# A two-block transformer kernel: a zeroed margin moved ahead of the loads, pooling read some ticks after GpSimd starts it, and the sums of w_ada spread differently over three stages

## The chip, the cores and the metric

The kernel runs on 1 core of one Trainium2 chip, as one launch. Its time is the device time of the whole program in microseconds (us); smaller is better. Before the change the median of 3 runs is 2774.2 us (2769.51 to 2774.95).

## The reference, cut to what matters

All arrays are float32, batch 1, 256 tokens, model width 2048. Two different transformer blocks run one after the other, each once.

```
h = rms_norm(x, pre_mix_g);  q, k, v, u = split(h @ w_in)        # 4 x 1024 columns
a = chunked_attention(q, k, v, rel_bias)                         # 8 heads of 128
p = multiscale_pool(u): group g = 0..3 (256 channels each):
        trailing mean over 2, 4, 8, 16 tokens, minus the token;  then @ pool_w[g], * pool_scale
x = x + rms_norm(concat(a, p) @ w_o)
x = x + rms_norm((gelu(conv(h @ w_up)[:5632]) * conv(..)[5632:]) @ w_down)   # first feed-forward

shift1, scale1, gate1, shift2, scale2, gate2 = split(silu(c) @ w_ada + b_ada, 6)     # also for c_ctx
hc = rms_norm(ctx) * (1 + cscale1) + cshift1;   h = rms_norm(x) * (1 + scale1) + shift1
keys and values from hc and h (512 rows), queries and gates from h (256 rows)
x = x + gate1 * merge(two attentions);  x = x + gate2 * swiglu(rms_norm(x) * (1 + scale2) + shift2)
```

w_ada is 2048 x 12288. Its product with a vector is computed on VectorE as dot products of rows, not on TensorE.

## The kernel before, in words

**Tokens and weights.** A float32 product is made of three matmuls on a rounded high part and a low part. Each weight slab is 128 x 1024 (512 KB, two half slabs): SyncE loads it into one of 4 tiles `w`, ScalarE casts it to `h` (L237), VectorE subtracts to get `l` (L238), both with 5 buffers, and TensorE uses it. `Stream.prep` issues these for the next slab as soon as TensorE's uses of the oldest one stand in the program. Every engine works through its own queue strictly in the order in which the Python code calls it, so this order is written out by hand.

**Side work.** Everything else in a stage (heads, pooling, norms) is written as generators in `Side`. A *tick* comes after each half slab; on a tick, at most `per` of the active generators that are due go on to their next `yield n`, which asks to be left alone for n ticks. At most `limit` are active, the rest wait in a queue.

**The sums of w_ada.** `Stream.vitems` holds 192 loads of 128 x 1024 of w_ada into two tiles `v` (L211, GpSimd's queue), and VectorE makes dot products of each with a broadcast row of silu(c) that lies in `adat` (L536, called a sum here). The first 64 loads have two sums each (c and c_ctx: "kind 0", 128 sums), then 32 loads each for shift2, gate1, scale2, gate2 with one sum each. `Stream.done` adds `pace` to a credit after each half slab and takes one sum per whole credit, up to `limit` loads; `PACE` has a pair per stage (feature-major and token-major products). After a sum that was a tile's last, the tile's next load is issued at once behind it. `ada_begin` loads the rows (L510) and lets the first sum come 8 ticks later.

**Block 1** (`block1`): norm of x, then v, q, k for heads 0 to 3 (`qkproj`), u (`uproj`), the other halves, pooling's mixing (`mix`), and the output projection. VectorE copies a zeroed margin of `ut` into the zero parts of the probabilities (L654). GpSimd's queue loads the condition `cc`, sends its silu to DRAM (`crow`, L626), loads the rows, then the table of biases `rb`, sets a part of the table to -1e30 (L651) and clears the margin (L652). `pool(g)` adds shifted copies on GpSimd (L666; 1, 2, 3, 4 additions for g = 0..3), and directly behind them VectorE corrects the start, scales, subtracts and splits (L669 to L676).

**First feed-forward** (`ffn1`): six groups of hidden columns, and in `ctx_norm` the norm of the context, which begins when kind 0 is summed. **Keys' stage** (start of `block2`): six chunks of 512 columns over four row tiles with 7 banks of PSUM; keys (chunks 0, 2, 3) are normed on VectorE (L1159 to L1190) before their bank is free. Then come queries, attention, merging and the second feed-forward.

Of the kernel before, what the change touches and what calls it, by code (L numbers as in the profile page):

```python
# [22 lines left out]
AF = mybir.ActivationFunctionType  # L23
# [3 lines left out]
P = 128  # L27
# [5 lines left out]
GROUPS = [range(g, min(g + 8, NFB)) for g in range(0, NFB, 8)]  # L33
NEG = -1e30

PACE = ((0.3, 0.35), (0.19, 0.33), (0.0, 0.88), (0.0, 0.3), (0.1, 0.13))

ROWS = 8

# [231 lines left out]
class Kernel:  # L271
# [275 lines left out]
    def ada_end(self, names, kind):  # L547
        nc = self.nc
        if names[0] == "gate":
            self.side.urgent.append((self.side.now + 3, lambda: self.gate_row(kind)))  # L550
            return
        for name, dst, g in (("sc1", self.g1, "norm1_g"), ("csc1", self.gc1, "norm1_g"), ("sc2", self.g2, "norm2_g")):
            if name in names or any(name in n for n in names):
                nc.vector.scalar_tensor_tensor(dst, self.ada_v[name], 1.0, self.vec(g), op0=ALU.add, op1=ALU.mult)
        self.ada_done.update(range(4 * kind, 4 * kind + 4 * len(names)))
# [41 lines left out]
    def block1(self):  # L597
# [22 lines left out]
        self.meet(self.norm_b(start(0), 0, hh, hl))  # L620
        xs1 = start(1)
        first = self.token_major([(hh, hl, 0), (hh, hl, 1)], self.staged(lambda: self.norm_t(xs1, 1, hh, hl)))
        cc = self.small[:32]
        nc.gpsimd.dma_start(cc, a["cc"])
        nc.scalar.activation(cc, cc, AF.Silu)
        nc.gpsimd.dma_start(self.crow.rearrange("o (j p) -> (o j) p", p=P), cc)  # L626
        self.pace = PACE[0]
        self.ada_begin({0: 0, 1: 2}, 64)

        _, ah, al = self.pair(2)  # L630
        qk = self.slot(4, F32R).rearrange("p (s k t) -> p s k t", s=4, k=4)
# [13 lines left out]
        def half():  # L645
            zk[0] += 1
            return xq[2 + zk[0] % 2]
        self.half = half
        nc.gpsimd.dma_start(tab, a["rb"])
        nc.gpsimd.dma_start(inv, a["inv"])  # L650
        nc.gpsimd.memset(tab[0:64, :, 192:256], NEG)  # L651
        nc.gpsimd.memset(ut[:, :, :16], 0.0)  # L652
        for i in range(4):
            nc.vector.tensor_copy(pt[:, i % 2, i // 2, 1, :P], ut[:, :8, :16])  # L654

        def pool(g):

            w = 2 ** (g + 1)
            src = ut[:, 2 * g:2 * g + 2, :]
            cur, step = src, 1  # L660
            bufs = [pa, pb]
            while step < w:
                dst = bufs.pop(0)
                bufs.append(dst)
                n = 2 * step - 1
                nc.gpsimd.tensor_add(dst[:, :, n:], cur[:, :, n:], cur[:, :, n - step:272 - step])  # L666
                cur, step = dst, 2 * step
            fix = self.stat(32).rearrange("p (k t) -> p k t", k=2)
            nc.vector.tensor_mul(fix, cur[:, :, 16:32], inv[:, g * 16:(g + 1) * 16].unsqueeze(1).to_broadcast([P, 2, 16]))  # L669
            m = bufs[0]  # L670
            nc.vector.tensor_scalar_mul(m[:, :, 32:], cur[:, :, 32:], 1.0 / w)
            nc.vector.tensor_copy(m[:, :, 16:32], fix)
            nc.vector.tensor_sub(m[:, :, 16:], m[:, :, 16:], src[:, :, 16:])
            ph, pl = pooled(g)
            nc.scalar.copy(ph, m[:, :, 16:])
            nc.vector.tensor_sub(pl, m[:, :, 16:], ph.bitcast(F32))  # L676
            pool_done.add(g)
            yield 1
# [85 lines left out]
            state["v"] += 1  # L764

        vout(first)
        qkproj(0)
        qkproj(1)
        state["qk"] = 1
# [146 lines left out]
    def ffn1(self, pair, x, mid):  # L916
# [58 lines left out]
        def chunk_end(gi, c, t, bank):  # L975
            if gi == 2 and c == t == 0:
                side.add(self.ctx_norm(ch, cl))
            last = gi == len(GROUPS) - 1
            yc = y[:, t, c * 512:(c + 1) * 512]
            if gi == 0:  # L980
                nc.scalar.copy(yc, bank)
            else:
                nc.vector.tensor_add(yc, bank, yc)
            if last:
                self.sumsq(yc, ss[t][:, c:c + 1])
                nc.vector.tensor_mul(yc, yc, self.pfg[c])
            if gi == len(GROUPS) - 2 and c == 3 and t == 1:
                side.drain()
                S.finish()
                side.drain()  # L990
                assert S.vdone == 64 and len(self.ada_done) == 8
                for n in range(4):
                    nc.gpsimd.dma_start(self.pfg[n], a["pfg"][:, n * 512:(n + 1) * 512].to_broadcast([P, 512]))
            if last and c == 3 and t == 1:
                self.gtop = self.gbase + 1024 + 2048
                xs8 = [self.xs_[:, :512], self.xs_[:, 512:]] + [self.g(512) for _ in range(6)]
                S.fill()
                side.add(normed(xs8))
# [116 lines left out]
    def block2(self):  # L1115
# [49 lines left out]
        for c in range(6):  # L1165
            if c == 0:
                banks = self.token_major(toks, [
                    self.seg(range(8)), self.seg(range(8, KB), (0, 1), True, after=lambda: side.until(lambda: 0 in self.normed)),
                    self.seg(range(8, KB), (2,), True, after=lambda: (side.until(lambda: 1 in self.normed), side.add(tables()))),
                    self.seg(range(8, KB), (3,)), self.seg(range(8), (2, 3))])  # L1170
                side.until(lambda: "done" in tabs)
                used = [(self.oi + i) % 4 for i in range(1, 5)]
                self.obanks, self.sbanks, self.oi = used + [4, 5, 6], [7], 3
                self.pace = PACE[2]
                self.ada_begin({0: 0, 1: 1}, 128)
                (qtab_a, qtab_b), (ktab_a, ktab_b) = tabs["q"], tabs["k"]
            else:
                banks = self.token_major(toks, [self.seg(range(KB), range(4))])
            is_k, hd = c in (0, 2, 3), 128 if c < 2 else 64
            v = lambda z: z.rearrange("p (h d) -> p h d", d=hd)  # L1180
            rk = [heads_ss(banks[0], hd, hd, 1.0 / hd)] if is_k else None
            for i in range(4):
                if is_k and i < 3:
                    rk.append(heads_ss(banks[i + 1], hd, hd, 1.0 / hd))
                out = tmp()
                if not is_k:
                    nc.scalar.copy(out, banks[i])
                else:
                    y = tmp()
                    nc.vector.tensor_mul(v(y), v(banks[i]), rk[i].unsqueeze(2).to_broadcast([P, 512 // hd, hd]))  # L1190
                    if i < 2:
                        gn = self.hg[:, 128:256] if hd == 128 else self.hg[:, 320:384]
                        nc.vector.tensor_mul(v(out), v(y), gn.unsqueeze(1).to_broadcast([P, 512 // hd, hd]))
                    else:
                        self.rope(out, y, ktab_a if hd == 128 else ktab_b, i - 2, hd, tmp())
                nc.gpsimd.dma_start(kv[c][:, i, :], out)
# [383 lines left out]
```

## Time and profile before

| | us |
|---|---|
| median of 3 runs (lowest, highest) | 2774.2 (2769.51, 2774.95) |
| the profiled execution | 2776.85 |
| its span, first to last instruction | 2775.1 |
| TensorE (PE) busy with matmuls | 2699.4 (97%) |
| VectorE (DVE) busy | 2015.8 (73%) |
| ScalarE (ACT) busy | 1336.8 (48%) |
| GpSimd (POOL) busy | 248.8 (9%) |
| mean granted TensorE clock | 0.993 |

How to read it: the rows shown further down are whole lines of the profile. Times are us from the span's start unless marked ns. Idle time in front of an instruction stands in brackets with the engine, tile and line that ended it. Matmul records overlap, so a busy PE is not a PE at its peak; a granted clock (PEclk) of 1.00 is 2.4 GHz, and while it is 0.50 the array runs at 1.2 GHz. L12 is line 12 of the kernel.

### The profile page before, as it was taken

Reading aid. Unit: us, or ns where it says so; the run is one execution under the profiler, and the core shown is the slowest. Engines: PE = TensorE matmul, PEld = TensorE weight load, DVE = VectorE, ACT = ScalarE, POOL = GpSimd, SP = SyncE. Lnnn points to the kernel's source line nnn. Section 1 sums busy time; section 2 is a strip of 40 time slices with the busy share of each in tenths; the row PEclk is TensorE's granted clock in tenths of the full one; section 3 lists DMA queues with packets and bytes.
Section 4 is the critical chain, followed back from the end, with each engine's and each line's share of the span. In section 5 each row is a group of like instructions: output and inputs, shape, how many; then the busy total and the mean of one; then the engine's idle time right before and its main releaser. Section 6 shows DMA issues by size and latency. Waiting matters only on the chain.

```text
span 2775.1 us, 36806 instructions
## 1 busy us (share of the span) xinstructions
PE 2699.4 (97%) x13654; PEld 2274.2 (82%) x13654; DVE 2015.8 (73%) x2938; ACT 1336.8 (48%) x1994; POOL 248.8 (9%) x395
## 2 busy tenths in 40 slices
PE   7989899999999999998999999999999999999999
PEld 6878788888888887777777788888878888888887
DVE  5878787888887767767577877778766666665566
ACT  5444455545455645321256655644454444444443
POOL 1010000000000000222211100011000000000000
PEclk9999999999999999999999999999999999999999
DMA  7666667676776765666855544489857777766565
GB/s 264 199 217 230 241 211 259 220 251 215 244 238 207 227 191 168 232 245 243 292 178 178 171 155 156 148 322 322 274 170 227 236 230 233 234 198 195 185 205 166
DMA packets 167573, 608.91 MB, mean 219 GB/s; under 512 B 19472, under 2 KB 19664, under 8 KB 166368
## 3 DMA queue, kind: packets, MB, share of 16 engines
q1 hardware_dynamic: 127728, 461.43, 49.6%
q0 software_dynamic: 39520, 144.87, 15.8%
q8 instruction: 107, 1.75, 0.3%
q14 instruction: 74, 0.61, 0.1%
q10 hardware_dynamic: 144, 0.25, 0.0%
HBM read 591.76 MB, written 14.71 MB: 219 GB/s over the span
## 4 chain that ended last, share of the span: by engine, by line
PE 78%; DVE 3%; DMA 3%; ACT 2%; issue 2%; POOL 0%; DVEq 0%; ACTq 0%; POOLq 0%
PE bank L359 34%; PE bank L392 14%; PE bank L393 13%; PE bank L395 13%; DMA v<-wada 3%; PE bank L342 1%; DVE l L238 1%; PE bank L343 1%; PE bank L344 1%; PE bank L1275 1%; ACT h L237 1%; DMA G<-kv 0%; ACT G L477 0%; PE bank L452 0%; DVE G L536 0%
## 5 line engine op out<-in xcount | busy, mean ns | idle before, releaser
L238 DVE TENSOR_TENSOR l<-w,h 128x1024 fp32r<-128x1024 f32 x870 | 1059.9, 1225 | 357.6 <-ACT h L237 346.8
L237 ACT CAST h<-w 128x1024 fp32r<-128x1024 f32 x870 | 908.9, 1051 | 615.8 <-PE bank L393 430.9
L359 PE MATMUL bank<-pair,h 128*128 128x512 f32 x3072 | 842.8, 395 | 6.5 <-DVE slot L338 3.5
L359 PEld LDWEIGHTS bank<-pair,h 128*128 128x128 f32 x3072 | 526.7, 189 | 76.4 <-issue 3.7
L392 PE MATMUL bank<-h,pair 128*128 128x512 f32 x1344 | 539.3, 401 | 24.1 <-DVE slot L1190 10.3
L393 PE MATMUL bank<-h,pair 128*128 128x512 f32 x1344 | 530.0, 394 | 2.1 <-DVE G L426 1.4
L359 PEld LDWEIGHTS bank<-pair,l 128*128 128x128 f32 x3072 | 470.1, 189 | 66.6 <-DVE l L238 0.8
L359 PE MATMUL bank<-pair,l 128*128 128x256 f32 x3072 | 488.1, 281 | 0.1
L395 PE MATMUL bank<-l,pair 128*128 128x512 f32 x1344 | 416.0, 395 | 6.0 <-DVE l L238 5.9
L536 DVE CUSTOM_DVE_ANT_0 G<-v,G 128x1024 bf16<-128x1024 f32 x256 | 327.8, 1280 | 70.5 <-DMA v<-wada 68.8
L392 PEld LDWEIGHTS bank<-h,pair 128*128 128x128 f32 x1344 | 256.5, 191 | 83.5 <-issue 16.3
L395 PEld LDWEIGHTS bank<-l,pair 128*128 128x128 f32 x1344 | 255.3, 190 | 64.0 <-DVE l L238 9.5
L393 PEld LDWEIGHTS bank<-h,pair 128*128 128x128 f32 x1344 | 256.3, 191 | 53.6 <-DVE G L426 1.8
L392 PE MATMUL bank<-h,slot 128*128 128x512 f32 x768 | 299.1, 390 | 1.0 <-ACT slot L337 1.0
L393 PE MATMUL bank<-h,slot 128*128 128x512 f32 x768 | 299.0, 389 | 0.0
L395 PE MATMUL bank<-l,slot 128*128 128x512 f32 x768 | 237.7, 389 | 0.0
L211 POOL DMA_DIRECT2D v<-wada x192 | 102.1, 532 | 1337.7 <-DVE G L536 1281.0
L367 ACT COPY G<-bank 128x256 f32<-128x256 f32 x192 | 71.6, 373 | 278.5 <-PE bank L359 278.2
L392 PEld LDWEIGHTS bank<-h,slot 128*128 128x128 f32 x768 | 144.2, 188 | 30.8 <-ACT slot L337 1.5
L393 PEld LDWEIGHTS bank<-h,slot 128*128 128x128 f32 x768 | 144.2, 188 | 30.4 <-DVE slot L338 0.5
L395 PEld LDWEIGHTS bank<-l,slot 128*128 128x128 f32 x768 | 144.1, 188 | 30.0
L368 DVE TENSOR_TENSOR G<-bank,G 128x256 f32<-128x256 f32 x192 | 81.1, 422 | 109.4 <-ACT G L367 109.1
(217 smaller groups left out, 1700.4 us busy)
## 6 DMA issues: line engine op xcount, KB each, us to landing
v<-wada POOLq DMA_DIRECT2D x192, 512.0 KB, 4.8
w<-wup SPq DMA_DIRECT2D x176, 512.0 KB, 4.3
w<-wgu SPq DMA_DIRECT2D x176, 512.0 KB, 4.0
w<-wdn SPq DMA_DIRECT2D x88, 512.0 KB, 4.5
w<-wfd SPq DMA_DIRECT2D x88, 512.0 KB, 4.1
w<-w SPq DMA_DIRECT2D x66, 512.0 KB, 4.5
w<-w2g SPq DMA_DIRECT2D x64, 512.0 KB, 3.5
w<-w2kv SPq DMA_DIRECT2D x52, 512.0 KB, 4.4
```

Of the source, the lines that this page charges most:

```text
L211: self.nc.gpsimd.dma_start(t, src)
L237: self.nc.scalar.copy(h, w)
L238: self.nc.vector.tensor_sub(l, w, h.bitcast(F32))
L342: t.matmul(out, ah, bh, start=start, stop=False)
L343: t.matmul(out, ah, bl, start=False, stop=False)
L359: t.matmul(bank[:, :size], w[:, j * P:(j + 1) * P], x[:, kb, :size], start=s == n == 0, stop=s == 3 and n == 7)
L367: self.nc.scalar.copy(z, bank[:, 256:])
L368: self.nc.vector.tensor_add(out, bank[:, :256], z)
L392: self.nc.tensor.matmul(banks[i], xh, h, start=seen[i] == 1, stop=False)
L393: self.nc.tensor.matmul(banks[i], xl, h, start=False, stop=False)
L395: self.nc.tensor.matmul(banks[i], xh, l, start=False, stop=seen[i] == total[i])
L536: nc.vector.tensor_tensor_reduce(out=self.junk.bitcast(mybir.dt.bfloat16), in0=w, in1=self.adat[:, slot * 1024:(slot + 1) * 1024], scale=1 ...
```

## The change

Four things are edited.

1. In block 1 the margin of `ut` is cleared first on GpSimd's queue, then the bias table is loaded; loading `cc`, its silu, sending it, the rows, and the -1e30 part move into a generator `side_rows` that runs beside `qkproj`.
2. `pool(g)` starts only when pool g-1 is done, and lets 2 + g ticks pass between GpSimd's additions and VectorE's part.
3. `PACE` of block 1 falls from (0.3, 0.35) to (0.2, 0.3), that of the first feed-forward rises from (0.19, 0.33) to (0.24, 0.36).
4. When kind 0 is done, `ada_begin` goes on with up to 24 loads of shift2 within the first feed-forward; the keys' stage gets pace (132 - loads done) / 80 in place of 0.88.

```
-PACE = ((0.3, 0.35), (0.19, 0.33), (0.0, 0.88), (0.0, 0.3), (0.1, 0.13))
+PACE = ((0.2, 0.3), (0.24, 0.36), None, (0.0, 0.3), (0.1, 0.13))
...
     def ada_end(self, names, kind):
+        if kind == 0:
+            self.ada_begin({0: 0, 1: 1}, 88)
...
     block1, behind the first product:
-        cc = self.small[:32]
-        nc.gpsimd.dma_start(cc, a["cc"])
-        nc.scalar.activation(cc, cc, AF.Silu)
-        nc.gpsimd.dma_start(self.crow.rearrange("o (j p) -> (o j) p", p=P), cc)
-        self.pace = PACE[0]
-        self.ada_begin({0: 0, 1: 2}, 64)
...
+        nc.gpsimd.memset(ut[:, :, :16], 0.0)
         nc.gpsimd.dma_start(tab, a["rb"])
         nc.gpsimd.dma_start(inv, a["inv"])
-        nc.gpsimd.memset(tab[0:64, :, 192:256], NEG)
-        nc.gpsimd.memset(ut[:, :, :16], 0.0)
...
+        def side_rows():
+            cc = self.small[:32]
+            nc.gpsimd.dma_start(cc, a["cc"])
+            yield 6
+            nc.scalar.activation(cc, cc, AF.Silu)
+            nc.gpsimd.dma_start(self.crow.rearrange("o (j p) -> (o j) p", p=P), cc)
+            self.pace = PACE[0]
+            self.ada_begin({0: 0, 1: 2}, 64)
+            nc.gpsimd.memset(tab[0:64, :, 192:256], NEG)
+            yield 1
...
         def pool(g):
+            while g and g - 1 not in pool_done:
+                yield 1
...
                 nc.gpsimd.tensor_add(dst[:, :, n:], cur[:, :, n:], cur[:, :, n - step:272 - step])
+            yield 2 + g
             fix = self.stat(32).rearrange("p (k t) -> p k t", k=2)
...
         vout(first)
+        side.add(side_rows())
         qkproj(0)
...
     ffn1, end of the last group but one:
                 side.drain()
+                S.limit = 64
                 S.finish()
                 side.drain()
+                S.limit = S.vdone
...
     keys' stage, chunk 0:
-                self.pace = PACE[2]
+                self.pace = 0.0, (132 - S.vdone) / 80
```

On GpSimd's queue at the start of block 1 the order was this (L624 and L626 are `cc` and its silu, L652 is the margin):

```order
L624 DMA G<-cc 32x128
L626 DMA crow<-G 32x128
L510 DMA G<-crow 128x1024 x2
L649 DMA slot_332<-rb 128x2048
L650 DMA G<-inv 128x64
L651 MEMSET slot_332 64x8x64
L652 MEMSET G 128x8x16
L211 DMA v_92<-wada 128x1024
```

and is now this (L645 is the margin, L654 and L657 are `cc` and its silu, L660 is the -1e30 part):

```order
L645 MEMSET G 128x8x16
L646 DMA slot_327<-rb 128x2048
L647 DMA G<-inv 128x64
L654 DMA G<-cc 32x128
L657 DMA crow<-G 32x128
L510 DMA G<-crow 128x1024 x2
L660 MEMSET slot_327 64x8x64
L211 DMA v_92<-wada 128x1024
```

The margin now has nothing in front of it that waits for the silu or for a load.

On VectorE's queue, pooling's second and third group stood directly behind one another (L669 to L676 are one group's part, L238 makes a slab's low part, L536 is a sum):

```order
L669 TENSOR_TENSOR G<-G 128x32
L671 TENSOR_SCALAR G<-G 128x2x240
L672 COPY G<-G 128x2x16
L673 TENSOR_TENSOR G<-G 128x2x256
L676 TENSOR_TENSOR pair_329<-G,pair_329 128x2x256
L238 TENSOR_TENSOR l_91<-w_81,h_86 128x1024
L368 TENSOR_TENSOR G<-bank_70,G 128x256
L536 ISA G<-v_93,G 128x1024
L536 ISA G 128x1
L669 TENSOR_TENSOR G<-G 128x32
```

and between the second and the third group's part there now stands this:

```order
L686 TENSOR_TENSOR pair_324<-G,pair_324 128x2x256
L368 TENSOR_TENSOR G<-bank_71,G 128x256
L238 TENSOR_TENSOR l_89<-w_80,h_84 128x1024
L536 ISA G<-v_92,G 128x1024
L536 ISA G 128x1
L238 TENSOR_TENSOR l_90<-w_81,h_85 128x1024
L368 TENSOR_TENSOR G<-bank_72,G 128x256
L238 TENSOR_TENSOR l_91<-w_78,h_86 128x1024
L679 TENSOR_TENSOR G<-G 128x32
```

Three slabs' low parts now come first instead of one. The last group's part stands behind the 48th slab's low part, in place of the 44th's; the first product that waits for pooling (`mix`) still comes 12 slabs later.

Counted over VectorE's queue, the sums that stand ahead of the n-th slab's low part are:

| slab | 34 | 50 | 110 | 270 | 350 | 390 | 430 |
|---|---|---|---|---|---|---|---|
| before | 10 | 21 | 55 | 126 | 128 | 144 | 192 |
| now | 6 | 13 | 41 | 127 | 152 | 161 | 192 |

Block 1 ends about slab 110, the first feed-forward about slab 360, the keys' stage about slab 425.

## Rows read from the trace of the kernel before

**Rows 1.** The page's first part: busy us, share of the span, instructions.

```profile
PE 2699.4 (97%) x13654; PEld 2274.2 (82%) x13654; DVE 2015.8 (73%) x2938; ACT 1336.8 (48%) x1994; POOL 248.8 (9%) x395
```

**Rows 2.** Waits of PE, whole span: us in total, times, longest us.

```profile
PE bank L392 <- DVE slot L1190: 10.3, 3, 7.5
...
PE bank L1264 <- DMA G<-kv: 3.8, 1, 3.8
PE bank L359 <- DVE slot L338: 3.5, 1, 3.5
PE bank L342 <- ACT slot L748: 2.7, 2, 1.4
...
PE bank L561 <- DVE G L536: 1.6, 1, 1.6
PE bank L359 <- ACT h L237: 1.5, 1, 1.5
PE bank L359 <- DVE pair L711: 1.5, 1, 1.5
```

**Rows 3.** Stretches: length, busy of PE, PEld, DVE, ACT, POOL; PEclk, DMA share, GB/s.

```profile
50.00:60.00 10.00, 6.55 (x31) 5.35 (x30) 6.05 (x11) 0.78 (x2) 1.70 (x4) 0.83 0.71 263
152.50:162.50 10.00, 9.95 (x33) 8.02 (x34) 7.71 (x10) 3.38 (x5) 2.60 (x3) 0.74 0.69 221
...
750.00:900.00 150.00, 150.00 (x807) 129.18 (x806) 114.44 (x171) 81.48 (x127) 9.48 (x16) 1.00 0.67 222
...
1228.00:1240.00 12.00, 9.86 (x37) 7.68 (x36) 8.46 (x17) 4.04 (x6) 7.78 (x6) 0.86 0.29 112
1276.00:1294.00 18.00, 10.51 (x36) 8.16 (x35) 13.39 (x27) 4.04 (x6) 9.45 (x9) 0.72 0.45 165
...
1372.00:1395.00 23.00, 17.61 (x73) 13.84 (x72) 11.86 (x14) 8.09 (x11) 5.25 (x9) 0.93 0.77 263
```

**Rows 4.** POOL and DVE in order of time, 40 to 54: start, us.

```profile
40.53 0.51 POOL L626 DMA_DIRECT2D crow<-G  x1 [19.07 <-ACT G L625]
...
53.26 0.52 POOL L651 MEMSET slot<- 64x512 f32 x1 [6.48 <-DMA slot<-rb]
...
53.95 0.63 DVE L654 CAST slot<-G 128x128 fp32r<-128x128 f32 x4 [14.09 <-POOL G L652]
```

**Rows 5.** Pooling: PE's wait in 100 to 340; line L666; POOL and DVE by time.

```profile
PE bank L392 <- ACT h L237: 7.7, 2, 5.7
...
L666 POOL TENSOR_TENSOR G<-G x10: 1072/1084/1997, 124.4 to 163.9; 128x542 f32<-128x542 f32 x4, 128x538 f32<-128x538 f32 x3, 128x530 f32<-128x530 f32 x2, 128x514 f32<-128x514 f32 x1
...
  DVE G L669: 11.4, 3
...
124.01 2.60 DVE L238 TENSOR_TENSOR l<-w,h 128x1024 fp32r<-128x1024 f32 x1
...
145.17 2.00 POOL L666 TENSOR_TENSOR G<-G 128x542 f32<-128x542 f32 x1 [4.76 <-DVE G L368]
```

**Rows 6.** Two of the page's costliest groups: count, busy us, mean ns, idle before.

```profile
L238 DVE TENSOR_TENSOR l<-w,h 128x1024 fp32r<-128x1024 f32 x870 | 1059.9, 1225 | 357.6 <-ACT h L237 346.8
...
L536 DVE CUSTOM_DVE_ANT_0 G<-v,G 128x1024 bf16<-128x1024 f32 x256 | 327.8, 1280 | 70.5 <-DMA v<-wada 68.8
```

**Rows 7.** DVE by time at the ends of chunks 2 and 3 of the keys' stage.

```profile
1229.29 0.69 DVE L1159 TENSOR_REDUCE G<-slot 128x8 f32<-128x512 f32 x1 [2.78 <-ACT slot L1158]
...
1279.83 1.28 DVE L536 CUSTOM_DVE_ANT_0 G<-v,G 128x1024 bf16<-128x1024 f32 x1 [3.28 <-DMA v<-wada]
```

**Rows 8.** The chain of waits at the end of the keys' stage: start, us, what.

```profile
1377.72 2.16 POOL kv L1196 x4
1379.88 9.37 DMA G<-kv
```

**Rows 9.** Waits in 360 to 1060; then loads of ctx, issue to landing.

```profile
DVE l L238 <- ACT h L237: 93.3, 110, 2.7
...
ACT G L477 <- DMA G<-ctx: 2.0, 2, 1.8
...
DMA to landing us min/median/max: 3.0/4.2/7.5
```

More of the change, by code (lines that the diff above doesn't have):

```diff
@@ L988, in chunk_end @@
                 side.drain()
+                S.limit = 64
                 S.finish()
                 side.drain()
-                assert S.vdone == 64 and len(self.ada_done) == 8
+                S.limit = S.vdone
+                assert len(self.ada_done) == 8
                 for n in range(4):
```

## The prediction

> **What bounds the kernel now.** I read the busy shares first: TensorE has matmuls in flight for 97% of the span [rows 1], so a change can only win what TensorE stands still or runs slow, and can lose wherever it makes an engine late that TensorE hardly waits for today. Then I read TensorE's waits over the whole span [rows 2]; the reader is to see that each line is a handful of waits, nearly all single places, with VectorE or what is queued behind it as releaser. The third view is the stretches around these places [rows 3]: PEclk below 1.00 there means that the array ran at 1.2 GHz for part of the stretch, just after TensorE had stood; (1 - PEclk) times the length is the clock time that is missing. Last came the queues of GpSimd and VectorE in order of time at each place [rows 4, 5, 7, 8].
>
> **The change part by part**, against the profiled execution of 2776.85 us (span 2775.1).
>
> *Margin first.* GpSimd stood 19.07 us for the silu of `cc`, later 6.48 us for the bias table, and only then cleared the margin; VectorE stood 14.09 us for it with its queue full of low parts behind [rows 4]. TensorE's bill is the 3.5 us wait on L338 [rows 2] and 0.17 x 10 = 1.7 us of missing clock behind it [rows 3]. Now the margin's clearing stands first, and nothing in front of it is slow, so the copies find it done. 3.5 + 1.7 = 5.2 us gained. What comes late next: the silu, the rows and the first sums, which nothing on TensorE reads. The bias table's load moves forward beside the first weight loads; if it delays these, TensorE's first slabs pay. Bounds 3 to 5.2; I take 5.2.
>
> *Pooling.* VectorE waited 11.4 us in three waits for GpSimd's additions [rows 5]; low parts behind them came late, and ScalarE's casts with them. TensorE paid 7.7 us in two waits [rows 5] and 1.5 in a third [rows 2], and 0.26 x 10 = 2.6 us of missing clock after the longest [rows 3]: 11.8 us. Now ticks lie in between, with up to three low parts in front of a group's correction. A tick is a half slab's eight matmuls, 8 x 150 / 807 = 1.5 us [rows 3], against 1.08 us for one addition [rows 5]; two to five ticks (3.0 to 7.5 us) cover one to four additions (1.1 to 4.3 us). The last group is done 12 slabs before TensorE needs it, so no wait takes this one's place there.
>
> But the additions are not free for VectorE. The one that ran beside a low part stretched it from 1.22 us to 2.60, and one that met a sum took 2.00 us in place of 1.08 [rows 5, 6]. The other eight ran while VectorE stood waiting for them, so their collisions were hidden in the wait; now VectorE works meanwhile. If all ten collide at about 1.1 us, VectorE loses 11 us, as much as the 11.4 of waits. Against that stand four sums fewer between slabs 34 and 50 (11 became 7 in the table of the change), 4 x 1.28 = 5.1 us [rows 6], and that the loss comes in pieces of 1 us, which the prepared slabs absorb, rather than in lumps of 3 to 5. Bounds of the gain 2 to 11.8; I take 2 us of remaining loss, a gain of 9.8.
>
> The Trainium skill has this as a rule ("SBUF — State Buffer", section "Who interferes with whom"): a VectorE instruction with two inputs in SBUF and a GpSimd instruction that reads SBUF shut each other out for the whole of the one that started first. The two stretched rows agree with it. By the rule alone, with every addition paid in full, this part would gain 2 us and the sum below would be 16.7; by the rows as I weigh them it is 24.5.
>
> *Fewer sums in block 1* (55 became 41 ahead of slab 110). The wait on L711 (1.5 us [rows 2]) had one sum between two halves of the mixing's evacuation; it is no longer there: 1.3 of the 1.5. Of the two waits on L748 (2.7 us) the second loses a sum in its chain, the first only has it moved: 1.2. Bounds 0 to 4.2; I take 2.5.
>
> *Keys' stage.* 64 sums become 40. A sum costs 1.28 us of VectorE and its `v` must land first; VectorE stood 68.8 us for these loads [rows 6], nearly all of it here, because 64 loads through two tiles leave a load less time than its round trip. That matters at a chunk's end: at chunk 3 VectorE stood 3.28 us for a `v` in front of the reductions that free the first bank; at chunk 2 it had nothing in front and waited for ScalarE instead [rows 7]. The two ends have the same work: 37 matmuls in 12 us around the one, 36 in 18 us around the other [rows 3]. The pace falls from 0.88 to 44 / 80 = 0.55 a half slab, so a load has 1.6 times as long to land, and the chunk 3 end should look like the chunk 2 end: 18 - 12 = 6 us gained (bounds 3 to 9). The last sum of gate1, for which TensorE waited 1.6 us (L561 [rows 2]), loses its lag on `v`: 1.5 (0 to 1.6). Then the first keys: TensorE waited 3.8 us [rows 2] and lost 0.07 x 23 = 1.6 us of clock [rows 3] for a read of 9.37 us, which GpSimd issued behind four writes that had been waiting behind the last `v` load [rows 8]. The writes now come 1 to 2 us sooner, the landing itself stays: 2 (0 to 5.4).
>
> *First feed-forward, where the sums go.* It takes 111 sums in place of 73: 38 x 1.28 = 49 us more on VectorE. TensorE does not stand there at all (150.00 of 150.00, and no wait of it in rows 2 lies there), and VectorE's idle time is waiting for ScalarE's casts, 93.3 us [rows 9], which themselves run as far ahead as the buffers let them. That is the cover. It is thinnest late: in 750 to 900 VectorE is 114 us busy with 10 sums, and about 21 of the 25 that the table now shows behind slab 270 make it 141 of 150 [rows 3]. There too the context's norm now meets the sums on GpSimd's queue: each of its 16 loads stands behind a `v` load that waits for a sum, so ScalarE, which waited only 2.0 us for them, may now wait a landing of 4.2 us for each of its eight squares [rows 9]. A slab takes 2775 / 870 = 3.2 us [rows 6], and four are prepared ahead, 12.8 us; two groups of four waits, 16.8 us each, would lose 2 x 4 = 8 us. Bounds 0 to 14, with 6 us for bursts on a 94% busy VectorE; I take 2.5 lost, near the free end, since loads of the first group can be issued together.
>
> *Sum.* 5.2 + 9.8 + 2.5 + 6 + 1.5 + 2 - 2.5 = 24.5 us. 2776.85 - 24.5 = 2752.4 for an execution like the profiled one; the median of the runs is 2.65 us lower, so 2749.7. I predict 2750.
>
> **The rivals.**
>
> *The collisions eat pooling's gain.* All ten additions hit VectorE in full, and it is as late as before. For it: the two rows with collisions; against it: fewer sums, and work that fits between. It gives 9.8 - 2 = 7.8 us less: 2758. Chance 0.17.
>
> *VectorE becomes the bound in the feed-forward.* 94% busy leaves little for catching up, and TensorE loses 14 us and some clock in place of 2.5, as it did at 140 to 155 in block 1. For it: the count; against it: TensorE has no wait there today. 2750 + 15 = 2765, at the edge of what can be told from no change. Chance 0.09.
>
> *Slower: the context's norm.* GpSimd's queue carries its loads behind `v` loads, and both ScalarE's squares and VectorE's scalings stand for each landing: 16 x 4.2 = 67 us, less 2 x 12.8 prepared, 42 us lost. The gains of 27 (the sum without the 2.5) turn into 15 lost: 2789. It decides when more than (27 + 25.6) / 4.2 = 12 of the 16 loads are waited for in full. Against it: the scalings have three ticks (4.5 us) between load and use. Chance 0.05.
>
> **How the numbers follow.** The forecast keeps 0.69. Its own terms at their good ends give 5.2 + 11.8 + 4.2 + 9 + 1.6 + 5.4 = 37, or 2737; with pooling at 2, the feed-forward at -14 and the rest as taken 5.2 + 2 + 2.5 + 6 + 1.5 + 2 - 14 = 5, or 2769. All good ends at once, or both bad ones, are unlikely: 2739 to 2767, which takes in the first two rivals. About 0.2% (5.5 us) is what a measurement here can tell from no change. Faster needs less than 2768.7: the forecast, the first rival and half of the second, less the tail, 0.87; same 0.08, from the second rival and the tail; slower 0.05.
>
> **What would show it.** Right: no wait of TensorE on L338 near 52 us and no VectorE wait for the margin; VectorE's wait for GpSimd's additions under 2 us in all, while low parts of 2 to 2.6 us appear beside them; TensorE's wait at the end of chunk 3 near 2 us, as at chunk 2; VectorE's waits for `v` from 68.8 to under 15 us. Wrong: TensorE's waits on `h` or `l` around 130 to 175 still adding up to 5 us or more; waits on `h`, `l` or `w` between 750 and 950, or ScalarE standing more than 15 us in all for `ctx`; the wait at chunk 3 staying above 5 us.

## The result, and the profile after

| | us | ratio to before, 95% interval |
|---|---|---|
| before, median of the same comparison | 2774.6 | |
| after, median of 4 runs (2794.85 to 2798.22) | 2796.6 | 1.0082 [1.0064, 1.0099] |
| after, profiled execution; its span | 2798.2; 2796.1 | |

The change made the kernel 22 us slower, where 24.5 us of gain were forecast. Both traces hold 13654 matmuls, so the places of gain and loss are found by comparing when the matmul with the same number starts (worked out from the two traces; a few transpositions stand at other places, which shifts a number by a microsecond or two):

| matmuls | us in before | after less before | what lies there |
|---|---|---|---|
| 0 to 250 | 11 to 67 | -5.2 | the margin |
| 250 to 1500 | 67 to 320 | -16.5 | block 1: pooling (-13.3), mixing and heads |
| 2000 to 2250 | 425 to 478 | +7.3 | the first feed-forward's first group |
| 4000 to 5000 | 805 to 992 | +48.5 | the context's norm, beside the feed-forward |
| 6000 to 7000 | 1215 to 1455 | -11.2 | the keys' stage |
| all others | | -1.9 | |

So nearly everything that was meant to become faster did (34.8 us in all, where 27 were forecast), and one stretch lost more than all of it. First the page's busy times and two of its groups, which answer to [rows 1, 6]: the work is the same, and VectorE's wait for `v` fell from 68.8 to 22.6 us.

```profile
PE 2709.5 (97%) x13654; PEld 2281.2 (82%) x13654; DVE 2017.0 (72%) x2938; ACT 1335.9 (48%) x1994; POOL 254.0 (9%) x397
...
L238 DVE TENSOR_TENSOR l<-w,h 128x1024 fp32r<-128x1024 f32 x870 | 1063.0, 1228 | 429.8 <-ACT h L237 418.9
...
L536 DVE CUSTOM_DVE_ANT_0 G<-v,G 128x1024 bf16<-128x1024 f32 x256 | 329.3, 1286 | 23.6 <-DMA v<-wada 22.6
```

Then the waits of PE over the whole span, against [rows 2]. The margin's wait on L338, the pooling's on L392, those of 3.8 us on `kv` and 1.6 us on L561 are no longer at the top; what stands there now is L452 and L359, with VectorE's scaling L892 and ScalarE's cast L237 as releasers, and both lie between 818 and 970 us. (Of the first line, 10.6 us are the start of the kernel.)

```profile
PE bank L452 <- DVE G L439: 15.8, 4, 10.6
PE bank L452 <- DVE G L892: 12.5, 4, 5.0
PE bank L359 <- ACT h L237: 11.8, 3, 5.9
PE bank L392 <- ACT slot L337: 7.2, 3, 3.8
...
PE bank L392 <- DVE slot L1203: 5.9, 3, 2.1
```

The stretches that answer to [rows 3], at the same work: the margin, the pooling, 750 to 900 of before, the ends of chunks 2 and 3, the first keys; and the context's norm as a whole and the new stall in the feed-forward. Columns as there.

```profile
44.50:54.50 10.00, 10.00 (x60) 8.77 (x59) 5.39 (x7) 5.82 (x9) 1.99 (x4) 1.00 0.69 217
139.00:149.00 10.00, 10.00 (x45) 8.26 (x45) 9.22 (x12) 3.53 (x6) 6.58 (x5) 1.00 0.59 213
746.00:896.00 150.00, 136.61 (x679) 115.15 (x678) 116.51 (x181) 69.61 (x110) 15.52 (x30) 0.94 0.72 242
820.00:970.00 150.00, 118.24 (x533) 97.65 (x533) 100.69 (x156) 58.86 (x97) 18.32 (x34) 0.87 0.65 221
1255.00:1267.00 12.00, 9.86 (x43) 7.86 (x42) 4.20 (x8) 4.05 (x6) 3.62 (x3) 0.98 0.34 122
1304.00:1316.00 12.00, 9.86 (x41) 7.78 (x40) 5.61 (x11) 4.05 (x6) 4.75 (x5) 0.93 0.39 129
1358.00:1381.00 23.00, 23.00 (x104) 19.02 (x103) 12.03 (x15) 6.58 (x8) 4.82 (x9) 1.00 0.78 265
420.00:430.00 10.00, 5.97 (x22) 4.21 (x21) 9.29 (x15) 4.79 (x6) 0.53 (x1) 0.84 0.59 199
```

In the fourth row VectorE is busy 100.69 of 150 us, less than in the undisturbed stretch of before (114.44): it is not full there, it waits. PEclk is 0.87: besides standing, the array ran part of the stretch at 1.2 GHz. TensorE stands 150 - 118.24 = 31.8 us in that row, so of the 48.5 us some 17 are, by this estimate, time at the lower clock. Whom everybody waits for shows in the waits of all engines between 800 and 970 us, against [rows 9]: ScalarE's wait for `ctx` grew from 2.0 to 38.2 us, and VectorE's scalings add 11.8. Below them are the ctx loads themselves (both lines, L883 and L890), from issue to landing: 5.1 us where it was 4.2.

```profile
POOL v L211 <- DVE G L536: 106.3, 18, 13.3
ACT G L477 <- DMA G<-ctx: 38.2, 6, 7.8
...
DVE l L238 <- ACT h L237: 23.0, 14, 6.6
```

```profile
L883 POOL DMA_DIRECT2D G<-ctx x8: 538/541/543, 800.3 to 930.0; - x8
L890 POOL DMA_DIRECT2D G<-ctx x8: 541/541/581, 835.3 to 982.2; - x8
...
  ACT G L477: 38.2, 6
  DVE G L892: 11.8, 3
...
DMA to landing us min/median/max: 3.2/5.1/8.6
```

A part of the same 38.2 us in order of time, on three engines between 905 and 925 us: GpSimd, ScalarE, VectorE (start, us; in brackets the idle time before and its releaser).

```profile
907.56 0.53 POOL L211 DMA_DIRECT2D v<-wada  x1 [10.60 <-DVE G L536]
908.07 0.54 POOL L883 DMA_DIRECT2D G<-ctx  x1
917.95 0.53 POOL L211 DMA_DIRECT2D v<-wada  x1 [9.33 <-DVE G L536]
918.47 0.54 POOL L883 DMA_DIRECT2D G<-ctx  x1
```

```profile
912.62 0.63 ACT L477 ACTIVATE G<-G 128x512 f32<-128x512 f32 x1 [4.84 <-DMA G<-ctx]
...
913.25 1.03 ACT L237 CAST h<-w 128x1024 fp32r<-128x1024 f32 x1
...
923.55 0.63 ACT L477 ACTIVATE G<-G 128x512 f32<-128x512 f32 x1 [7.83 <-DMA G<-ctx]
```

```profile
914.31 1.23 DVE L238 TENSOR_TENSOR l<-w,h 128x1024 fp32r<-128x1024 f32 x1 [5.20 <-ACT h L237]
...
916.37 1.28 DVE L536 CUSTOM_DVE_ANT_0 G<-v,G 128x1024 bf16<-128x1024 f32 x1
917.57 0.08 DVE L536 DVE_READ_ACCUMULATOR2_ANT G<- 128x1 f32 x1
917.57 1.22 DVE L238 TENSOR_TENSOR l<-w,h 128x1024 fp32r<-128x1024 f32 x1
```

It is a ring. The ctx load at 908.07 was queued behind a `v` load; ScalarE's square waits for it (912.62), with the next casts behind the square; VectorE's low part waits for the cast (914.31); the sum behind that low part ends at 917.6 and only then frees the tile for the next `v` load (917.95), behind which the next ctx load stands (918.47). This turn takes 10.4 us (the next two, by GpSimd's queue, 11.5 and 11.8), and VectorE gets two low parts through in it (914.31, 917.57), work for two slabs of 3.2 us on TensorE: by this estimate some 4 us lost in the turn.

### The profile page after: what moved, and what is told of

It is laid out like the page before. It is cut to its first block, busy times and chain, and to the rows that moved or that the text cites. A ratio compares the mean times of both kernels' runs of the same rounds, so it can differ in the third digit from the quotient of the medians.

```text
span 2796.1 us, 36791 instructions
## 1 busy us (share of the span) xinstructions
PE 2709.5 (97%) x13654; PEld 2281.2 (82%) x13654; DVE 2017.0 (72%) x2938; ACT 1335.9 (48%) x1994; POOL 254.0 (9%) x397
## 4 chain that ended last, share of the span: by engine, by line
PE 74%; DVE 6%; issue 4%; ACT 3%; DMA 2%; POOL 1%; ACTq 0%; DVEq 0%; POOLq 0%
PE bank L359 29%; PE bank L392 14%; PE bank L393 14%; PE bank L395 14%; DVE l L238 2%; DMA G<-ctx 1%; ACT h L237 1%; DVE G L536 1%; PE bank L342 1%; PE bank L343 1%; PE bank L344 1%; PE bank L1288 1%; PE bank L452 0%; ACT G L477 0%; ACT G L459 0%
## 5 line engine op out<-in xcount | busy, mean ns | idle before, releaser
L238 DVE TENSOR_TENSOR l<-w,h 128x1024 fp32r<-128x1024 f32 x870 | 1063.0, 1228 | 429.8 <-ACT h L237 418.9
L237 ACT CAST h<-w 128x1024 fp32r<-128x1024 f32 x870 | 908.4, 1051 | 591.8 <-PE bank L393 408.7
L359 PE MATMUL bank<-pair,h 128*128 128x512 f32 x3072 | 847.6, 397 | 11.8 <-ACT h L237 11.8
L359 PEld LDWEIGHTS bank<-pair,h 128*128 128x128 f32 x3072 | 529.4, 190 | 82.4 <-ACT h L237 12.6
L392 PE MATMUL bank<-h,pair 128*128 128x512 f32 x1344 | 535.4, 398 | 11.3 <-DVE slot L1203 5.9
L359 PEld LDWEIGHTS bank<-pair,l 128*128 128x128 f32 x3072 | 472.6, 189 | 66.9 <-DVE l L238 0.4
L359 PE MATMUL bank<-pair,l 128*128 128x256 f32 x3072 | 489.9, 281 | 0.0
L536 DVE CUSTOM_DVE_ANT_0 G<-v,G 128x1024 bf16<-128x1024 f32 x256 | 329.3, 1286 | 23.6 <-DMA v<-wada 22.6
L392 PE MATMUL bank<-h,slot 128*128 128x512 f32 x768 | 303.2, 395 | 10.6 <-ACT slot L337 7.2
L392 PEld LDWEIGHTS bank<-h,pair 128*128 128x128 f32 x1344 | 253.9, 189 | 69.6 <-issue 12.9
L393 PE MATMUL bank<-h,slot 128*128 128x512 f32 x768 | 302.5, 394 | 2.0 <-DVE slot L338 2.0
L392 PEld LDWEIGHTS bank<-h,slot 128*128 128x128 f32 x768 | 146.3, 191 | 42.2 <-ACT slot L337 8.5
```

The lines of the kernel that those rows point to most:

```text
L237: self.nc.scalar.copy(h, w)
L238: self.nc.vector.tensor_sub(l, w, h.bitcast(F32))
L359: t.matmul(bank[:, :size], w[:, j * P:(j + 1) * P], x[:, kb, :size], start=s == n == 0, stop=s == 3 and n == 7)
L392: self.nc.tensor.matmul(banks[i], xh, h, start=seen[i] == 1, stop=False)
L393: self.nc.tensor.matmul(banks[i], xl, h, start=False, stop=False)
L536: nc.vector.tensor_tensor_reduce(out=self.junk.bitcast(mybir.dt.bfloat16), in0=w, in1=self.adat[:, slot * 1024:(slot + 1) * 1024], scale=1 ...
```

## The experiments

Each is the changed kernel with the edit shown. The norm's stretch is how much more than in before passes between the starts of matmuls 4000 and 5000; in the changed kernel it is 48.5 us.

**The ctx loads on SyncE's queue** (both places):

```diff
-                nc.gpsimd.dma_start(z, cr[:, t, c * 512:(c + 1) * 512])
+                nc.sync.dma_start(z, cr[:, t, c * 512:(c + 1) * 512])
```

> The changed kernel with one edit: the sixteen loads of the context's norm are issued by SyncE in place of GpSimd, so that none of them stands behind a v load. Theory Q (queue): the 48 us lost between 825 and 965 us come from a ring of waits, square <- ctx load <- v load ahead of it on GpSimd's queue <- w_ada sum that frees the v tile <- a VectorE instruction that waits for ScalarE <- square. Then the loss is gone but for what SyncE's own weight loads now hold up: 2748 us (2744 to 2757), ScalarE waits for ctx under 15 us in all (38 in the changed kernel). Theory V (VectorE is too full there, with about 25 sums beside the evacuations, whatever the queue does): no gain worth telling, 2785 to 2800. Theory L (lead: a load has only three ticks before it is used, on whatever queue): about half of the loss stays, 2765 to 2780.

2812.2 us, 1.0124 [1.0107, 1.0141]; the norm's stretch 64.7. A miss for all three theories: it got worse. SyncE's queue in order of time in that kernel:

```profile
904.78 0.61 SPq L883 DMA_DIRECT2D G<-ctx  x1
915.43 0.33 SPq L204 DMA_DIRECT2D w<-wup  x1
915.81 0.42 SPq L883 DMA_DIRECT2D G<-ctx  x1
923.91 3.58 SPq L204 DMA_DIRECT2D w<-wup  x2
927.54 0.42 SPq L883 DMA_DIRECT2D G<-ctx  x1
```

Each ctx load now stands behind a weight load, and a weight load waits for a `w` tile that VectorE frees: the same ring with another load in it. The loads shown still go out 11 to 12 us apart. The edit had changed the obstacle, not taken it away, so this run could not part the theories.

**Shorter sums.** `width` is 64 of 1024 columns for shift2's sums, so shift2 is not computed in full:

```diff
+                width = 64 if names[0] == "sh2" else 1024
...
-                    nc.vector.tensor_tensor_reduce(out=self.junk.bitcast(mybir.dt.bfloat16), in0=w,
-                                                   in1=self.adat[:, slot * 1024:(slot + 1) * 1024], scale=1.0,
+                    nc.vector.tensor_tensor_reduce(out=self.junk.bitcast(mybir.dt.bfloat16)[:, :width], in0=w[:, :width],
+                                                   in1=self.adat[:, slot * 1024:slot * 1024 + width], scale=1.0,
```

> The changed kernel with the sums of shift2 (the ones that it adds to the first feed-forward) cut to 64 of their 1024 columns, so that shift2 is not computed in full; loads, waits and the order of the instructions stay. A sum then takes some 0.2 us of VectorE in place of 1.28. Theory V: VectorE is no longer full, the 48 us are gone, about 2750. Theory Q: the v loads still stand in front of the ctx loads and wait for VectorE's turn, not for its 1.28 us, so most of the loss stays: 2780 to 2795.

2786.5 us, 1.0040 [1.0027, 1.0054]; the stretch 38.7. The line of the sums between 800 and 970 us in this kernel:

```profile
L538 DVE CUSTOM_DVE_ANT_0 G<-v,G x24: 274/278/285, 819.4 to 968.9; 128x64 bf16<-128x64 f32 x24
```

With 1.28 us each become 0.28, 24 us are taken from VectorE and 10 of the 48.5 come back, as theory Q had it. VectorE's fullness is not the main cause; whether its place in the ring is, the next runs have to show.

**More lead** between a ctx load and its use:

```diff
                 nc.gpsimd.dma_start(z, cr[:, t, c * 512:(c + 1) * 512])
+                yield 5
                 self.sumsq(z, ss[:, c:c + 1])
-                yield 3
+                yield 1
...
                 nc.gpsimd.dma_start(z, cr[:, t, c * 512:(c + 1) * 512])
-                yield 3
+                yield 5
                 nc.vector.tensor_scalar_mul(z, z, r)
```

> The changed kernel with the waits of the context's norm moved only: five ticks in place of none between a ctx load and the square that reads it, and five in place of three between a ctx load and its scaling; all sums, loads and queues stay. Theory L: a load that waits behind a v load lands in about 10 us, five ticks are some 8 to 16 us, so ScalarE no longer stands for ctx and the ring opens: 2750 to 2758. Theory V: stays at 2785 to 2800. Theory Q alone, if five ticks do not cover the time that a load stands in the queue: between, 2765 to 2780.

2763.2 us, 0.9958 [0.9943, 0.9972]; the stretch 20.0. That lies between what theories L and Q expected. Lead alone gives back 28.5 us and makes the kernel faster than before. What is left, in the waits between 818 and 970 us of this kernel, seems to be the queue, where a ctx load can still be held up past its five ticks; the run with the lead and ScalarE's queue together, further down, tests it.

```profile
ACT G L477 <- DMA G<-ctx: 17.6, 4, 9.4
...
PE bank L452 <- DVE G L893: 12.0, 4, 7.3
```

**The next 24 sums stay in the keys' stage:**

```diff
-        if kind == 0:
-            self.ada_begin({0: 0, 1: 1}, 88)
```

> The changed kernel without the part that starts the next 24 sums as soon as scale2 is done: they stay in the keys' stage (pace 68 sums over 80 half slabs, 0.85). The rest of the change stays. Theories Q, V and L alike: no sum is left at the context's norm, so the 48 us are gone, and the 11 us won in the keys' stage go back: 2796.6 - 48 + 11 = about 2759 (2752 to 2764). If the loss at the context's norm is not of the sums at all (its own order, the clock), it stays: 2795 or more.

2754.8 us, 0.9927 [0.9912, 0.9942]; the stretch 0.1. That the loss is these sums' doing is shown. The keys' stage then gains only 3.5 us (11.2 in the changed kernel), with gate1's last sum late, as this wait of PE in the keys' stage shows:

```profile
PE bank L561 <- DVE G L536: 7.1, 1, 7.1
```

**Sums held while the norm runs:**

```diff
+        self.S.hold = 1 << 30
         for t in range(2):
...
+        self.S.hold = 0
```

> The changed kernel with its sums held back while the context's norm runs (no sum and no v load between the norm's first load and its last transposition; they go on behind it). Seen so far, by the start of the same matmul: the norm's stretch (matmul 4000 to 5000) costs 48.5 us in the changed kernel, 64.7 with the ctx loads on SyncE, 38.7 with short sums, 20.0 with five ticks of lead, and nothing with no sums there. Theory (sums beside the norm cost all of it, the same number of sums behind the norm costs nothing): 2796.6 - 48.5 = 2748 (2744 to 2754), the keys' stage as in the changed kernel. Rival (VectorE has no room for them behind the norm either): stalls move to 950 to 1060 us and the time is 2760 or more.

2751.7 us, 0.9913 [0.9898, 0.9928]; the stretch 2.8, and the keys' stage gains 13.9. Not all of the 24 sums follow behind the norm: 14 do, between 950 and 1008 us, closer together than the 24 of the changed kernel (821 to 980 us), and ten are left to the keys' stage, so the expectation's "same number of sums behind the norm" is tested by these 14 only. They cost nearly nothing: from 810 to 1010 us this kernel's TensorE runs at full clock, with VectorE busier than in the changed kernel (154.24 against 143.00 us).

```profile
810.00:1010.00 200.00, 198.19 (x1027) 168.52 (x1026) 154.24 (x232) 111.02 (x173) 15.35 (x29) 1.00 0.70 234
```

**Lead and shorter sums together** (the two edits above; shift2 again not in full):

> Five ticks of lead for the ctx loads and shift2's sums cut to 64 of 1024 columns (shift2 is not computed in full). Theory (two causes that add: the lead is worth 28 us of the 48.5, the sums' own VectorE time 10): the norm's stretch costs 10 us (5 to 13) in place of the 20.0 with the lead alone, 2750 to 2757. Rival (what is left with the lead is the place of the v loads in front of the ctx loads, not VectorE's time): it stays at 17 to 21, 2760 to 2765.

2754.8 us, 0.9926 [0.9911, 0.9941]; the stretch 8.8, as the theory of two adding causes had it. Which of a sum's two effects is at work, VectorE's time or the sooner freed `v` tile, this run does not say; the one with ScalarE's queue and lead does.

**The pooling without its ticks:**

```diff
-            while g and g - 1 not in pool_done:
-                yield 1
...
-            yield 2 + g
```

> The changed kernel with the pooling as before: no ticks between GpSimd's additions and VectorE's correction. It tells apart what gained 13.3 us between matmul 500 and 750 (109 to 169 us). Theory P (the ticks): VectorE waits for GpSimd again, 8 us or more in three waits, and 9 to 13 of the 13.3 us are given back, about 2807. Theory S (fewer sums beside the pooling, pace 0.2 and 0.3 for 0.3 and 0.35): at most 4 us are given back, 2797 to 2801.

2804.4 us, 1.0100 [1.0083, 1.0117]. Of the 13.3 us between matmuls 500 and 750 this gives 7.9 back, less than theory P expected and more than theory S; VectorE waits for GpSimd again, as in [rows 5]. So the ticks are worth 7.9 us, and the other 5.4 belong to the rest of the change. That these are the fewer sums is likely, but no run shows it. Waits between 105 and 180 us:

```profile
DVE G L676 <- POOL G L673: 10.7, 3, 5.0
...
PE bank L392 <- ACT h L237: 4.8, 2, 2.5
```

**The hold and a lower first pace:**

```diff
-PACE = ((0.2, 0.3), (0.24, 0.36), None, (0.0, 0.3), (0.1, 0.13))
+PACE = ((0.2, 0.3), (0.19, 0.36), None, (0.0, 0.3), (0.1, 0.13))
```

> As the kernel with the sums held during the context's norm, and the first pace of the first feed-forward 0.19 (as before) in place of 0.24; the second stays 0.36. The changed kernel stands 3.9 us at 423 us for a product's split and loses 3.4 us of clock behind it, 7.3 in all; VectorE had two sums and two low parts between the product and the split. Theory (the higher pace puts the second sum there): 7 us less than with the hold alone, 2741 (2737 to 2745). Rival (the stall is of the order of the casts, with either pace): the same as with the hold alone, within 2 us.

2757.5 us, 0.9933 [0.9919, 0.9948]: a miss. Between matmuls 2000 and 2250 it still loses 5.2 us (6.1 with the hold alone). That does not clear the sums: at the lower pace two of them still stand between the last product's evacuation (419.92 us) and its split (426.94), at 421.93 and 424.60, so the run did not take away what it was to test. And the sums that the lower pace leaves for the keys' stage, 23 of the 24 in place of ten, make gate1's last one late again:

```profile
PE bank L563 <- DVE G L536: 5.9, 1, 5.9
```

**The hold, and no sum at the first group's turn:**

```diff
             if last or i < 2:
                 next(gen)
+            if i == 7 and half == 0:
+                S.hold = side.now + 8
```

> The sums held during the context's norm, and also for eight ticks from the last product of the first feed-forward's first group, so that none stands between that product's evacuation and its split; paces as in the changed kernel. Theory (the 3.9 us stall at 423 us is two sums in that chain): the stall goes with the clock behind it, 6 us, from 2751.7 to 2745.5 (2742 to 2749). Rival (the chain of casts alone is too late there since block 1 ends earlier): within 2 us of the kernel with the first hold alone, 2750 to 2754.

2748.6 us, 0.9907 [0.9893, 0.9922], the fastest, though its interval overlaps that of the hold alone, so the times alone do not part the theory from its rival. TensorE's standing near 423 us falls from 4.2 us in two waits (3.8 and 0.4, with the hold alone) to 1.9 (1.4 and 0.5), and the loss between matmuls 2000 and 2250 from 6.1 to 4.1. So the two sums between the last product and its split were 2 of the 6 us; the rest is not these sums, and stays open. The norm's stretch costs 6.0 here. The longer of the two waits that are left:

```profile
PE bank L392 <- ACT slot L337: 1.4, 1, 1.4
```

**The lead and ScalarE's queue together** (the lead's edit, and `nc.scalar.dma_start` in both places):

> Five ticks of lead, and the sixteen ctx loads issued by ScalarE, on whose queue no v load and no weight load stands. It says what the last 20.0 us of the norm's stretch are with the lead alone on GpSimd's queue. Theory Q (still the v loads in front of the ctx loads): the stretch costs 10 or less, 2750 to 2755. Theory V (VectorE's time, as the 7.5 us with short sums said): it stays at 17 to 21, 2760 to 2766.

2752.4 us, 0.9921 [0.9904, 0.9937]; the stretch 3.8. With the lead alone on GpSimd's queue it was 20.0: the remainder was the `v` loads in front, not VectorE's time, with every sum in full length. Nor is it how much VectorE or the DMA engines have to do: from 810 to 1010 us both are busier than in the changed kernel (165.55 against 143.00 us, 271 against 224 GB/s), and TensorE is at full clock.

```profile
810.00:1010.00 200.00, 198.03 (x1026) 168.26 (x1025) 165.55 (x250) 107.60 (x169) 16.63 (x30) 1.00 0.79 271
```

ScalarE's wait for `ctx` has gone from the list, and this is what is left of the norm's waits on PE:

```profile
PE bank L452 <- DVE G L893: 1.5, 2, 1.1
```

**ScalarE's queue alone:**

```diff
-                nc.gpsimd.dma_start(z, cr[:, t, c * 512:(c + 1) * 512])
+                nc.scalar.dma_start(z, cr[:, t, c * 512:(c + 1) * 512])
```

> The changed kernel with the sixteen ctx loads issued by ScalarE and no lead added: a square follows its load at once. No v load and no weight load stands in front of a ctx load. If the place on the queue is most of the loss: the stretch costs under 25 us of the 48.5, 2760 to 2773. If the missing lead is (each square stands for a whole landing of 3 to 5 us on any queue, and everything on ScalarE behind it): 35 to 65, 2783 to 2813, as on SyncE.

2775.6 us, 1.0006 [0.9997, 1.0015]; the stretch 29.5, between the two expectations. No `v` load and no weight load stands in front of a load any more, and ScalarE's wait for it falls from 32.3 to 18.2 us between 818 and 970 us, but a square right behind its load still stands for the landing. The line of the changed kernel, then that of this one:

```profile
ACT G L477 <- DMA G<-ctx: 32.3, 5, 7.8
```

```profile
ACT G L477 <- DMA G<-ctx: 18.2, 5, 5.0
```

The stretches side by side: GpSimd's queue 48.5, with lead 20.0; ScalarE's queue 29.5, with lead 3.8. The lead is worth 28.5 or 25.7 us, the queue 19.0 or 16.2: two causes that nearly add, each with about the same price whichever is taken first. The landing itself differs little between the two queues (median from issue 5.1 and 4.7 us without lead, 5.7 and 5.4 with it), so it can hardly be what the queue's 16.2 us with lead are made of.

## Why the prediction was wrong

**The step that failed** is the first feed-forward, "I take 2.5 lost, near the free end, since loads of the first group can be issued together". It lost 48.5 us at the context's norm and 7.3 at its start. Four things were wrong in its account of the norm.

The price of a wait. The prediction took one landing, 4.2 us. The run has nine waits of 5.6 us on average (38.2 + 11.8 over 6 + 3), and in the ring shown above 10.4 us and more pass from one load to the next, because a load is not issued until the sum is done that itself stands behind ScalarE's wait. The prediction saw the queue's order but priced its links one by one, and did not see that they close.

The cover. The four prepared slabs are made by ScalarE's casts, and ScalarE is the engine that stands. ScalarE's first wait, 5.9 us up to 808 us, cost TensorE nothing; in its second, 4.6 us up to 828 us, TensorE already stood 3.3 us for a cast. So the slabs covered one wait and were not refilled before the next; the 12.8 us were counted for each group of four, as if the casts went on. TensorE's wait between 818 and 970 us:

```profile
PE bank L392 <- ACT h L237: 3.3, 1, 3.3
```

The clock. For the margin, the pooling and the first keys the prediction added the missing clock to the standing; for the norm, in its sum and in its third rival, it counted standing alone. Some 17 of the 48.5 us are clock.

The lead. "Issued together" is contradicted by the code: a square follows its load in the same tick, and three ticks pass before the next load. That could have been read from `ctx_norm`. The run with more lead shows what this was worth: 28.5 us.

**The rival that came true** is the third, "the context's norm": slower, at 2789, with the right place and the right queue. Its 42 us were near the 48.5 that came. But its point of decision, more than 12 of 16 loads waited for in full, was not reached: nine loads were enough, each dearer. That condition, worked out with the single landing, is why it got 0.05. So the place and the queue were foreseen; that the number came near is luck, with too many waits, each too cheap, and no clock. The second rival, a VectorE at its bound, is refuted at the norm: 100.69 of 150 us busy, and full-length sums cost 3.8 us there once the loads are out of their way. The prediction's own sign of being wrong, ScalarE standing more than 15 us in all for `ctx`, came with 38.2.

The 7.3 us at the feed-forward's first group are in no term by name; only the 6 us for bursts in the bound allow for them. Two sums in one chain are 2 of them; the cause of the rest stays open.

**What was right.** The margin: 5.2 us forecast, 5.2 found, and TensorE's stretch at full clock. The keys' stage: 9.5 forecast (6 + 1.5 + 2), 11.2 found (12.4 to 13.9 in those runs that have the same number of sums there, so one trace is good to about 2 us); chunk 3's end now looks like chunk 2's (9.86 us busy of 12 in both rows). The first keys were under-sized: 2 was taken of 0 to 5.4, and the wait on `kv` fell from 3.8 to 0.9 us with the clock at 1.00, nearly the upper end. VectorE's wait for `v` fell to 22.6 us, not under the 15 that were to show it. PE's waits from 1200 to 1500 us:

```profile
PE bank L392 <- DVE slot L1203: 4.3, 2, 2.1
...
PE bank L1277 <- DMA G<-kv: 0.9, 1, 0.9
```

**Right in mechanism, wrong in size.** The pooling: 9.8 forecast, with the four fewer sums beside it counted in, and 13.3 found, above the bound of 11.8. The missing clock had been read too small: the row from 152.5 us starts after the clock had fallen, and from 149 to 159 us it is 0.66, 3.4 us in place of 2.6. And the 2 us of remaining loss did not come. The run without the ticks gives 7.9 of the 13.3 to the ticks. The fewer sums at their two places behind it: 2.5 forecast, about 3.2 found. The wait on L711 is gone, but near 185 us two others stand in its place (1.4 and 0.4 us, on L342), so 1.3 forecast became nothing; the second wait on L748, 1.3 us at 251 us, is gone together with the clock behind it, 3.7 us between matmuls 1000 and 1250 where 1.2 were forecast. The sum of both terms, 12.3, was 4.2 us too small.

The collisions went as forecast in kind: GpSimd's ten additions have a median of 1772 ns where it was 1084, and the low parts and sums beside them are longer. POOL's and DVE's rows of the changed kernel:

```profile
139.05 3.96 POOL L675 TENSOR_TENSOR G<-G 128x538 f32<-128x538 f32 x2
```

```profile
138.26 1.79 DVE L238 TENSOR_TENSOR l<-w,h 128x1024 fp32r<-128x1024 f32 x1 [0.19 <-ACT h L237]
139.97 2.10 DVE L536 CUSTOM_DVE_ANT_0 G<-v,G 128x1024 bf16<-128x1024 f32 x1
...
142.00 2.08 DVE L238 TENSOR_TENSOR l<-w,h 128x1024 fp32r<-128x1024 f32 x1
```

Two additions took 3.96 us, and 1.28 and 1.22 us of VectorE became 2.10 and 2.08. Six low parts and two sums were lengthened between 113 and 156 us, 6.2 us of VectorE in all, in pieces of 0.2 to 1.0 us; TensorE's clock in that stretch is 1.00 and it does not stand. The first rival is refuted: the price on VectorE was no price on TensorE. Alone, two additions of 1.08 us and VectorE's three instructions of 1.22, 1.28 and 1.22 would make 5.9 us; together they took from 138.26 to 144.08 us, 5.8, as if they went by turns. The Trainium skill's rule on the shared port ("SBUF — State Buffer", section "Who interferes with whom") agrees with this.

On the queues the Trainium skill ("DMA: Bandwidth & Descriptors", section "Issuing engines are not separate DMA queues") says that starting transfers from several engines only saves the time to initiate them. No run here tests that for bandwidth. What the choice of the engine changed in this kernel is more than that time: the same 16 loads, begun by ScalarE in place of GpSimd, were worth 19.0 us, since another instruction that waits stands in front of them.

## What to carry to other kernels

Where a change puts a load that waits for a result into a queue, list what stands behind it there and follow each of those back to the waiting one: if the chain closes, a turn costs the sum of its links, and buffers filled by an engine inside the ring covered only its first wait here. Moving a load to another queue helps only if nothing that waits stands there either; issuing it several ticks ahead of its use, or keeping the other loads off the queue while it runs, did more here. And a rival whose price is as large as all the gains deserves a look at the code that decides it before it gets a small chance.

## What was not expected of the hardware

Ten additions that collide with VectorE's instructions stretched both sides, by up to 1.08 us on GpSimd (1085 to 2162 ns) and 1.03 us on VectorE (a sum of 2.31 us), without TensorE losing anything. That the stretch near 423 us still loses some 4 us when the two sums are taken from it, 1.9 of them standing, is not explained by these runs.
